# A hybrid MLA and GLA step on one core: decode's products in whole groups, and the prompt's P v in two products with the row sums on GpSimd

## The chip, the cores and the metric

The kernel runs on one core of a Trainium2 chip. The metric is the device time of one execution in microseconds (us), as the median of several runs. The core has five engines that each take their own instructions in order: PE (TensorE, matrix products; its weight loads are listed apart as PEld), DVE (VectorE), ACT (ScalarE), POOL (GpSimd) and SP (SyncE, which issues most of the transfers). They wait for each other by semaphores. Products land in PSUM, a small memory of 8 banks of 128 x 512 f32 numbers, everything else is in SBUF.

## The reference

One layer of a decoder runs for a prompt of 2048 tokens and for 8 sequences of 8 new tokens with 4096 cached positions each. The parts that matter here are the two attentions of the MLA heads:

```python
# prompt: 8 heads, 64 + 32 wide queries and keys, 64 wide values, causal
s = (jnp.einsum('bqhd,bkhd->bhqk', qn_b, k_nope)
     + jnp.einsum('bqhr,bkr->bhqk', qr_b, k_rope)).astype(jnp.float32) * scale
s = jnp.where(kpos[None, :] <= qpos[:, None], s, -jnp.inf)
p = jax.nn.softmax(s, axis=-1).astype(v.dtype)
return jnp.einsum('bhqk,bkhd->bqhd', p, v)

# decode, per sequence: pages of 128 cached latents (128 wide) and rotary keys (32 wide)
c = jnp.concatenate([ckv_pool[pages].reshape(-1, KV_LORA), cn.astype(ckv_pool.dtype)], axis=0)
kr = jnp.concatenate([kr_pool[pages].reshape(-1, QK_ROPE), krn.astype(kr_pool.dtype)], axis=0)
s = (jnp.einsum('thc,lc->htl', ql, c)
     + jnp.einsum('thr,lr->htl', qr, kr)).astype(jnp.float32) * scale
s = jnp.where(mask[None], s, -jnp.inf)
p = jax.nn.softmax(s, axis=-1).astype(c.dtype)
return jnp.einsum('htl,lc->thc', p, c)
```

Around them stand the input projection, the gated linear attention (GLA), the gates, the output projection, a second gated projection and the norms.

## The kernel before

The program is a sequence of stages: the input projection (up to about 354 us), GLA (to about 753 us), then the prompt's attention with decode woven in (to about 1183 us), the prompt's attention alone (to about 1394 us), its last head, among which the output's weights are already loaded and split (to about 1467 us), and the output.

Products in f32 precision are made of products of a faster type, `fp32r`. A number is split into a leading part, which is the number as written in that type, and a rest (`split`: ACT or GpSimd writes the leading part, DVE subtracts it, at L59 and L60; the helper `gcopy` at L51 is the GpSimd form). A product is then three products: leading by leading, leading by rest, rest by leading.

**The prompt's attention** (`attention`) goes head by head, and in a head unit by unit, j = 3, 2, 1, 0. A unit is 512 queries against their 4j + 4 blocks of 128 keys, one block a step. There are 40 steps to a head. The last four of each unit are on the diagonal: they cover 512, 384, 256 and 128 of the queries and are masked. A step is:

- three products of keys and queries into one PSUM tile `psC` (L940, L941, L942), of which there are two;
- two exponentials by ACT from it, into `ph` as the leading part of P (L944) and into `pf` in full (L946);
- a subtraction by DVE, `pl` = `pf` − `ph` (L948), both read from SBUF;
- on the diagonal two selects by GpSimd, which zero the masked part of `ph` and `pl` (L951);
- three products into the unit's tile `poC`, one bank of PSUM: leading values and a block of 64 columns of ones by `ph` (L953), the values' rest by `ph` (L954), leading values and ones by `pl` (L955). Rows 0 to 63 of `poC` are the output, and rows 64 to 127, by the ones, the sums of P over the keys.

A tile `VT` holds, for each key block, 64 columns of the values' rest, 64 of their leading part and 64 of ones. Between the steps of one unit stand the products, reductions and the transposition that find the row maxima of the next one (L910; DVE's L912, L915, L917; L925, L926). At a unit's end ACT copies `poC` out (L958), and the output and the sums go to memory (`Od`, `Dd`). The sums are later read back as `rcC`, inverted and written as `Rd`. The output stage reads this, and GpSimd multiplies it onto the gates (L1067).

**Decode** (`decode`) goes in 16 chunks, two for each of 8 sequences. A chunk's cached latents are loaded twice, by pages through SP (`ct`, and `kt` for the rotary keys) and row by row by indirect transfers that GpSimd issues (`cr`, L760). A chunk then is: four products of latents (L768) and two of rotary keys (L771) into a tile `ptD` of two banks; DVE's maximum (L774); ACT's exponential over 1024 columns (L779); eight transposes into the next `ptD` (L789); copies out of it, half by ACT (L792) and half by DVE (L793); 16 products P by latents into `poD` (L798). In the trace each product of decode is two records, a transpose one. `ptD` and `poD` have one buffer each. PSUM's eight banks are so shared as 2 (`ptD`), 1 (`poD`), 2 (`pmC`, the maxima), 2 (`psC`) and 1 (`poC`).

What sets the order: both attentions are generators, advanced in turn at a fixed rate. The framework then schedules all instructions by its own model of the machine's time and emits one fixed order for each engine. A wait on an engine therefore holds all that stands behind it.

## Time and profile before

| | us |
|---|---|
| runs (3) | 1921.84 median, 1916.32 to 1924.11 |
| profiled execution, own time | 1924.76 |
| its span | 1923.0 |
| stage: attention with decode, 753 to 1183 | 430 |
| stage: attention alone, 1183 to 1394 | 211 |
| stage: last head, 1394 to 1467 | 73 |
| stage: output, 1467 to 1923 | 456 |
| PE / DVE / ACT / POOL busy over the span | 1792.7 / 1093.2 / 777.2 / 472.6 |

The mean granted PE clock of the profiled execution is 0.959 of full speed. In the rows of the profile, L940 is line 940 of the kernel. A group's row tells line, engine, operation, the tiles it writes and reads with shapes, and its count; then its busy time in us and the mean of one in ns; then how long the engine stood idle ahead of these instructions, and for what. Products overlap on PE, so the mean of one is longer than the distance from one to the next. The stages' limits were read from the timeline.

### The profile page before, as it was taken

What the parts mean: (1) busy time and instruction counts of PE and PEld (TensorE: products, weight loads), DVE (VectorE), ACT (ScalarE), POOL (GpSimd) and SP (SyncE); (2) the same over time, 40 slices, a digit from 0 to 9 for tenths busy, and PEclk for the clock granted to TensorE, in tenths of its full rate; (3) what the DMA queues carried; (4) which work ended last, traced back from release to release, by engine and by line L of the source; (5) the groups of instructions that cost most, each with busy time, mean ns of one, the idle gap of its engine ahead of it and who ended that gap; (6) DMA issues with size and microseconds to landing.
All of it is one profiled execution on the core that took longest, in us unless ns stands there. A gap on an engine that the chain in (4) does not pass through costs nothing.

```text
span 1923.0 us, 27575 instructions
## 1 busy us (share of the span) xinstructions
PE 1792.7 (93%) x8928; PEld 1367.0 (71%) x8928; DVE 1093.2 (57%) x2373; ACT 777.2 (40%) x1896; POOL 472.6 (25%) x851
## 2 busy tenths in 40 slices
PE   4999987899999995997999999999998999999997
PEld 3877776688777784564665657777776888888885
DVE  6366566566734766555655667777786433333324
ACT  4354455344332432352543546666662122212112
POOL 5263342334433332121021111111126200000000
PEclk7999999899989998898998999999998999999999
DMA  5164476511111107446344452233134332222210
GB/s 167 47 228 164 145 262 212 136 39 38 48 34 41 45 23 184 155 124 171 106 131 128 121 160 64 72 86 75 44 102 139 102 94 82 85 81 79 77 48 33
DMA packets 197994, 200.56 MB, mean 104 GB/s; under 512 B 26362, under 2 KB 141932, under 8 KB 197852
## 3 DMA queue, kind: packets, MB, share of 16 engines
q1 hardware_dynamic: 193244, 182.03, 32.4%
q0 software_dynamic: 4608, 16.78, 2.7%
q8 instruction: 71, 1.16, 0.3%
q14 instruction: 71, 0.58, 0.1%
HBM read 142.39 MB, written 56.35 MB: 103 GB/s over the span
## 4 chain that ended last, share of the span: by engine, by line
PE 69%; DMA 4%; DVE 3%; issue 1%; POOL 1%; SPq 1%; ACT 1%; POOLq 0%; ACTq 0%; DVEq 0%
PE pgE L63 7%; PE pgE L65 7%; PE pgE L64 7%; PE pgB L65 4%; PE pgB L63 4%; PE pgB L64 4%; PE psC L940 3%; PE poC L953 3%; PE poC L955 3%; PE pmC L910 3%; PE psC L941 3%; PE psC L942 3%; PE poC L954 3%; PE ptD L768 2%; PE poD L798 2%; PE ptD L771 1%
## 5 line engine op out<-in xcount | busy, mean ns | idle before, releaser
L944 ACT ACTIVATE ph<-psC 128x512 fp32r<-128x512 f32 (+1 forms) x320 | 171.6, 536 | 262.4 <-PE psC L942 187.9
L948 DVE TENSOR_TENSOR pl<-pf,ph 128x512 fp32r<-128x512 f32 (+1 forms) x320 | 192.0, 609 | 69.7 <-ACT pf L946 63.5
L946 ACT ACTIVATE pf<-psC 128x512 f32<-128x512 f32 (+1 forms) x320 | 170.5, 533 | 0.0
L912 DVE TENSOR_REDUCE mxC<-pmC 128x1 f32<-128x512 f32 x192 | 129.1, 684 | 66.0 <-PE pmC L910 65.2
L951 POOL TENSOR_SCALAR_AFFINE_SELECT ph<-ph 128x128 fp32r<-128x128 f32 x128 | 44.7, 349 | 429.3 <-DVE pl L948 322.3
L953 PE MATMUL poC<-ph,VT 128*128 128x512 f32 (+1 forms) x320 | 125.9, 393 | 9.1 <-POOL ph L951 7.4
L910 PE MATMUL pmC<-KT,qC 96*128 96x512 f32 (+2 forms) x320 | 121.4, 403 | 8.5 <-issue 4.1
L940 PE MATMUL psC<-qC,KT 97*128 97x512 f32 (+1 forms) x320 | 126.3, 395 | 2.0 <-ACT pf L946 1.2
L955 PE MATMUL poC<-pl,VT 128*128 128x512 f32 (+1 forms) x320 | 123.5, 387 | 1.8 <-DVE pl L948 1.5
L941 PE MATMUL psC<-qC,KT 96*128 96x512 f32 (+1 forms) x320 | 120.1, 375 | 0.0
L942 PE MATMUL psC<-qC,KT 96*128 96x512 f32 (+1 forms) x320 | 119.7, 374 | 0.0
L954 PE MATMUL poC<-ph,VT 128*64 128x512 f32 (+1 forms) x320 | 117.6, 368 | 0.0
L953 PEld LDWEIGHTS poC<-ph,VT 128*128 128x128 f32 x320 | 62.1, 194 | 40.4 <-POOL ph L951 14.0
L64 PE MATMUL pgE<-wpg,hh 128*128 128x512 f32 x224 | 87.7, 391 | 0.0
L63 PE MATMUL pgE<-wpg,hh 128*128 128x512 f32 x224 | 87.6, 391 | 0.0
L1124 DVE SCALAR_TENSOR_TENSOR thE<-thE,pgE 128x512 f32<-128x512 f32 x32 | 22.0, 687 | 114.3 <-ACT thE L1123 114.2
L910 PEld LDWEIGHTS pmC<-KT,qC 96*128 96x128 f32 x320 | 62.4, 198 | 33.9 <-issue 14.2
L940 PEld LDWEIGHTS psC<-qC,KT 97*128 97x128 f32 x320 | 62.0, 194 | 33.8 <-ACT pf L946 7.7
L65 PE MATMUL pgE<-wpg,hl 128*128 128x512 f32 x224 | 85.4, 392 | 0.0
L1123 ACT ACTIVATE thE<-pgE 128x512 f32<-128x512 f32 x32 | 19.1, 598 | 161.1 <-PE pgE L65 161.1
L955 PEld LDWEIGHTS poC<-pl,VT 128*128 128x128 f32 x320 | 61.9, 193 | 24.1 <-issue 5.9
L60 DVE TENSOR_TENSOR x<-x 128x512 fp32r<-128x512 f32 (+2 forms) x74 | 64.7, 920 | 22.2 <-PE pgB L64 14.1
(450 smaller groups left out, 4643.5 us busy)
## 6 DMA issues: line engine op xcount, KB each, us to landing
x<-in_xT SPq DMA_DIRECT2D x32, 512.0 KB
ct<-in_ckvT SPq DMA_DIRECT2D x256, 64.0 KB
x<-in_w_in SPq DMA_DIRECT2D x16, 512.0 KB
Qn<-qq SPq DMA_DIRECT2D x16, 512.0 KB
Kn<-qq SPq DMA_DIRECT2D x16, 512.0 KB
Vd<-qq SPq DMA_DIRECT2D x16, 512.0 KB
KT<-Kn SPq DMA_DIRECT2D x32, 256.0 KB
VT<-Vd SPq DMA_DIRECT2D x8, 1024.0 KB
```

The source lines that it names most:

```text
L63: T_.matmul(out, ah, bh, start=first, stop=False)
L64: T_.matmul(out, ah, bl, start=False, stop=False)
L65: T_.matmul(out, al, bh, start=False, stop=last)
L910: T_.matmul(ps[:, :w], qs, kv[0][cb][:96, 0, :w], start=True, stop=True)
L940: T_.matmul(ps[:, c0:], kh[:, ks], qh[:, c0:], start=True, stop=False)
L941: T_.matmul(ps[:, c0:], kh[:96, ks], ql[:, c0:], start=False, stop=False)
L942: T_.matmul(ps[:, c0:], kl[:, ks], qh[:96, c0:], start=False, stop=True)
L944: A.activation(ph[:, c0:], ps[:, c0:], AF.Exp, scale=SC)
L948: V.tensor_tensor(pl[:, c0:], pf[:, c0:], ph[:, c0:].bitcast(F32), op=ALU.subtract)
L953: T_.matmul(o[:, c0:], vt[:, kb, DV:192], ph[:, c0:], start=kb == 0, stop=False)
L954: T_.matmul(o[:DV, c0:], vt[:, kb, 0:DV], ph[:, c0:], start=False, stop=False)
L955: T_.matmul(o[:, c0:], vt[:, kb, DV:192], pl[:, c0:], start=False, stop=kb == nk - 1)
```

## The change

There are three parts.

**Decode.** A new helper, `together`, keeps the instructions of a group in the order in which they are written and asks for all but the first at high priority. Decode's six QK products, its eight transposes and its 16 P products are each written as such a group. The QK group's order of halves is reversed. The pool `poD` is gone: everything of decode that went there now takes a buffer of `ptD`, of which there is still one. The transposes are copied out by one ACT copy of 1024 columns.

**The prompt's attention.** `poC` is now two banks, still with one buffer. One product of a step is the whole of the values, rest and leading part, by `ph` into the first bank; the second is leading values and ones by `pl` into the second bank. The sums of `ph`, which the ones gave before, are made by GpSimd in a tile `sumC` (two buffers): a copy in a unit's first step, then one addition per step. The second exponential overwrites the scores in `psC`; `pf` is gone, and DVE subtracts with one operand in PSUM. At a unit's end ACT copies half of the first bank, DVE copies the second, DVE and GpSimd each make one addition of 64 rows, `sumC` is split, two products with ones sum it over the 128 partitions, and DVE adds the result to the row that goes to `Dd`.

**The output.** It has two buffers in place of three in the pool `ptE` and six in place of five in `pgE`.

```diff
+    def together(calls):
+
+        for n, f in enumerate(calls):
+            if n:
+                with tc.high_priority():
+                    tc.keep_in_program_order(f())
+            else:
+                f()
...
         pt = pool(c, "ptD", 1, PSUM)
-        po = pool(c, "poD", 1, PSUM)
...
         def chunk(b, ck, ct, kt, cr, mx, dn, oc):
             ps = pt.tile([P, 2, 512], F32, name="ptD")
-            for u in range(2):
-                for e in range(2):
-                    T_.matmul(ps[64 * e:64 * e + 64, u], flat(qlat[:, b]), ct[:, u, e], start=True, stop=False)
-            for u in range(2):
+
+            def latent(u, e):
+                return T_.matmul(ps[64 * e:64 * e + 64, u], flat(qlat[:, b]), ct[:, u, e], start=True, stop=False)
+
+            def rope(u):
                 rows = slice(64 * u, 64 * u + 64)
-                T_.matmul(ps[:, u], qrs[rows, b].rearrange("p e h t -> p (e h t)"), kt[rows], start=False, stop=True)
+                return T_.matmul(ps[:, u], qrs[rows, b].rearrange("p e h t -> p (e h t)"), kt[rows], start=False, stop=True)
+
+
+            together([partial(latent, u, e) for u in (1, 0) for e in (1, 0)] + [partial(rope, u) for u in (1, 0)])
             yield
...
-            for k in range(8):
-                T_.transpose(tp[:, k * P:(k + 1) * P], sv[:, k], ident)
+            together([partial(T_.transpose, tp[:, k * P:(k + 1) * P], sv[:, k], ident) for k in range(8)])
             pT = sp.tile([P, 8, 2, SD], F32, name="pT")
-            pv = pT.rearrange("p k e q -> p (k e q)")
-            A.activation(pv[:, :512], tp[:, :512], AF.Copy)
-            V.tensor_copy(pv[:, 512:], tp[:, 512:])
+            A.activation(pT.rearrange("p k e q -> p (k e q)"), tp, AF.Copy)
             yield
-            oo = po.tile([P, 512], F32, name="poD")
-            for k in range(8):
-                for e in range(2):
-                    T_.matmul(oo[64 * e:64 * e + 64, :CL], pT[:, k, e], cr[:, e, k], start=k == 0, stop=k == 7)
+            oo = pt.tile([P, 2, 512], F32, name="ptD")[:, 0]
+            together([partial(T_.matmul, oo[64 * e:64 * e + 64, :CL], pT[:, k, e], cr[:, e, k], start=k == 0, stop=k == 7)
+                      for k in range(8) for e in range(2)])
...
         def attend(h, j, kv, q):
             (kt, vt), qt = kv, q
             qh, ql = qt[:, 0], qt[:96, 1]
-            o = po.tile([P, 512], F32, name="poC")
+            o = po.tile([P, 2, 512], F32, name="poC")
+            sm = sp.tile([P, 512], F32, name="sumC")
             nk = 4 * j + 4
...
                 A.activation(ph[:, c0:], ps[:, c0:], AF.Exp, scale=SC)
-                pf = pp.tile([P, 512], F32, name="pf")
-                A.activation(pf[:, c0:], ps[:, c0:], AF.Exp, scale=SC)
+                A.activation(ps[:, c0:], ps[:, c0:], AF.Exp, scale=SC)
                 pl = pp.tile([P, 512], F32R, name="pl")
-                V.tensor_tensor(pl[:, c0:], pf[:, c0:], ph[:, c0:].bitcast(F32), op=ALU.subtract)
+                V.tensor_tensor(pl[:, c0:], ps[:, c0:], ph[:, c0:].bitcast(F32), op=ALU.subtract)
...
-                T_.matmul(o[:, c0:], vt[:, kb, DV:192], ph[:, c0:], start=kb == 0, stop=False)
-                T_.matmul(o[:DV, c0:], vt[:, kb, 0:DV], ph[:, c0:], start=False, stop=False)
-                T_.matmul(o[:, c0:], vt[:, kb, DV:192], pl[:, c0:], start=False, stop=kb == nk - 1)
+                T_.matmul(o[:, 0, c0:], vt[:, kb, 0:P], ph[:, c0:], start=kb == 0, stop=kb == nk - 1)
+                T_.matmul(o[:, 1, c0:], vt[:, kb, DV:192], pl[:, c0:], start=kb == 0, stop=kb == nk - 1)
+
+                if kb == 0:
+                    gcopy(sm, ph.bitcast(F32))
+                else:
+                    G.tensor_tensor(sm[:, c0:], sm[:, c0:], ph[:, c0:].bitcast(F32), op=ALU.add)
                 yield
             ob = sp.tile([P, 512], F32, name="ob")
-            A.activation(ob, o, AF.Copy)
+            A.activation(ob[:DV], o[DV:P, 0], AF.Copy)
+            oc = sp.tile([P, 512], F32, name="oc")
+            V.tensor_copy(oc, o[:, 1])
+            V.tensor_tensor(ob[:DV], ob[:DV], o[:DV, 0], op=ALU.add)
+            G.tensor_tensor(ob[:DV], ob[:DV], oc[:DV], op=ALU.add)
             nc.sync.dma_start(Od[h * DV:(h + 1) * DV, j * 512:j * 512 + 512], ob[:DV])
-            nc.sync.dma_start(Dd[h:h + 1, j * 512:j * 512 + 512], ob[DV:DV + 1])
+
+            sr = sp.tile([P, 2, 512], F32R, name="sr", bufs=1)
+            split(sr[:, 0], sr[:, 1], sm)
+            st = pm.tile([P, 512], F32, name="pmC")
+            for l in range(2):
+                T_.matmul(st[:DV], vt[:, 0, P:192], sr[:, l], start=l == 0, stop=l == 1)
+            V.tensor_tensor(oc[DV:DV + 1], oc[DV:DV + 1], st[0:1], op=ALU.add)
+            nc.sync.dma_start(Dd[h:h + 1, j * 512:j * 512 + 512], oc[DV:DV + 1])
...
-            pt = pool(c, "ptE", 3, PSUM)
+            pt = pool(c, "ptE", 2, PSUM)
...
-            pg = pool(c, "pgE", 5, PSUM)
+            pg = pool(c, "pgE", 6, PSUM)
```

The framework moves the instructions accordingly. Up to about 753 us the order is the same on each engine. The lines of the changed kernel are about ten higher: L940 to L942 are L950 to L952, L953 is L962, L955 is L963, L768 and L771 are L777 and L781, L910 is L919, L951 is L960, L51 is L52, L1067 is L1091; L82 is the product that `together` calls, L968 the addition to `sumC`, and L975 the addition of 64 rows.

First, PE where decode's QK products of one chunk stand among attention, before (in brackets the semaphores that an instruction waits for):

```order
L798 MATMUL poD<-cr,pT 64x128 x3
L768 MATMUL ptD<-ct,qlat 64x512 [waits DMAHW4_49,DMAHW2_49,DMAHW6_49,DMAHW0_49,PE_49]
L768 MATMUL ptD<-ct,qlat 64x512 [waits DMAHW4_49,DMAHW6_49,DMAHW2_49,DMAHW0_49]
L768 MATMUL ptD<-ct,qlat 64x512
L940 MATMUL psC<-qC,KT_6769 128x512 [waits Activation_49]
L941 MATMUL psC<-qC,KT_6769 128x512
L942 MATMUL psC<-qC,KT_6769 128x512
L768 MATMUL ptD<-ct,qlat 64x512 [waits DMAHW4_49,DMAHW6_49,DMAHW2_49,DMAHW0_49]
L771 MATMUL ptD<-kt,qrs 128x512 [waits DMAHW5_49,DMAHW7_49,DMAHW3_49,DMAHW1_49] x2
```

and the like place after:

```order
L963 MATMUL poC<-pl,VT_6777 128x512 [waits DVE_49]
L950 MATMUL psC<-qC,KT_6770 128x512
L951 MATMUL psC<-qC,KT_6770 128x512
L952 MATMUL psC<-qC,KT_6770 128x512
L777 MATMUL ptD<-ct,qlat 64x512 [waits DMAHW4_49,DMAHW2_49,DMAHW6_49,DMAHW0_49,DVE_49]
L777 MATMUL ptD<-ct,qlat 64x512 x3
L781 MATMUL ptD<-kt,qrs 128x512 [waits DMAHW5_49,DMAHW7_49,DMAHW3_49,DMAHW1_49]
L781 MATMUL ptD<-kt,qrs 128x512
```

The six products now stand together, and the first one waits for all of the latents, and for DVE.

Second, PE in attention alone, between full steps of a unit, before:

```order
L910 MATMUL pmC<-KT_6771,qC 128x512 [waits DVE_49]
L955 MATMUL poC<-pl,VT_6778 128x512 [waits DVE_49]
L953 MATMUL poC<-ph,VT_6778 128x512 [waits Activation_49]
L954 MATMUL poC<-ph,VT_6778 64x512
L940 MATMUL psC<-qC,KT_6774 128x512 [waits Activation_49]
L941 MATMUL psC<-qC,KT_6774 128x512
L942 MATMUL psC<-qC,KT_6774 128x512
```

and after:

```order
L963 MATMUL poC<-pl,VT_6778 128x512 [waits DVE_49]
L962 MATMUL poC<-ph,VT_6778 128x512 [waits Activation_49]
L950 MATMUL psC<-qC,KT_6774 128x512
L951 MATMUL psC<-qC,KT_6774 128x512
L952 MATMUL psC<-qC,KT_6774 128x512
L919 MATMUL pmC<-KT_6773,qC 128x512 [waits DVE_49]
L919 MATMUL pmC<-KT_6774,qC 128x384 [waits DVE_49,PE_49]
```

L954 is gone, and the QK products, which waited for ACT's second exponential, now have their wait in the product by `pl` ahead of them, which waits for DVE's subtraction.

Third, GpSimd in the last head, where a unit's selects and the multiplication of the gates (`raw`) stand, before:

```order
L951 AFFINE_SELECT ph<-ph 128x128 [waits DVE_49]
L951 AFFINE_SELECT pl<-pl 128x128 [waits PE_49]
L1067 TENSOR_TENSOR raw<-raw 128x512 [waits DMAHW6_49,DMAHW7_49,DMAHW2_49,DMAHW0_49]
L951 AFFINE_SELECT ph<-ph 128x128 [waits DVE_49,Pool_49]
L951 AFFINE_SELECT pl<-pl 128x128 [waits PE_49,Pool_49]
```

and after:

```order
L968 TENSOR_TENSOR sumC<-sumC,ph 128x512 [waits Activation_49,Pool_49]
L975 TENSOR_TENSOR ob<-ob,oc 64x512 [waits DMAHW0_49,DVE_49]
L968 TENSOR_TENSOR sumC<-sumC,ph 128x512 [waits Activation_49,Pool_49] x5
L1091 TENSOR_TENSOR raw<-raw 128x512 [waits DMAHW5_49,DMAHW4_49,DMAHW3_49]
L968 TENSOR_TENSOR sumC<-sumC,ph 128x512 [waits Activation_49,Pool_49]
L960 AFFINE_SELECT ph<-ph 128x128 [waits DVE_49]
L960 AFFINE_SELECT pl<-pl 128x128 [waits PE_49]
```

The multiplication, which waits for transfers, now also has additions to `sumC` behind it in GpSimd's queue, and these share the queue with the selects.

13 lines of the change are left out of this document (7 added, 6 removed).

## The prediction

> **What bounds the kernel now.** I read the page's totals first, then the busy time by stage, then the groups and the timeline of the attention stage, then the chain of waits where decode runs. Totals:
>
> ```profile
> span 1923.0 us, 27575 instructions
> PE 1792.7 (93%) x8928; PEld 1367.0 (71%) x8928; DVE 1093.2 (57%) x2373; ACT 777.2 (40%) x1896; POOL 472.6 (25%) x851
> ```
>
> PE is busy 93% of the span. By stage (stretch, its length, then busy time and count of PE, PEld, DVE, ACT, POOL, then PE's granted clock, DMA share, GB/s): decode among attention, attention alone, the last head, the output.
>
> ```profile
> 753.00:1183.00 430.00, 398.91 (x1982) 249.53 (x1983) 254.79 (x755) 187.90 (x411) 60.81 (x136) 0.92 0.47 133
> 1183.00:1394.00 211.00, 207.74 (x1046) 164.84 (x1045) 161.73 (x415) 144.35 (x307) 33.52 (x120) 1.00 0.28 70
> 1394.00:1467.00 73.00, 64.10 (x278) 48.04 (x276) 54.56 (x115) 42.44 (x90) 27.81 (x48) 0.90 0.33 95
> 1467.00:1923.00 456.00, 442.05 (x1998) 358.73 (x1997) 171.05 (x243) 89.88 (x189) 52.13 (x88) 0.98 0.28 82
> ```
>
> Attention alone is PE's: 207.74 of 211 us (98%). In the decode stage PE has 31 us idle and a clock of 0.92. The output stage is PE's too. How many attention steps (one key block of one unit) fall in each of the first three stretches, the same view of L953's matmuls tells, one per step:
>
> ```profile
> 753.00:1183.00 430.00, 57.90 (x141) 27.44 (x142) 0.92 0.47 133
> 1183.00:1394.00 211.00, 51.25 (x139) 26.17 (x139) 1.00 0.28 70
> 1394.00:1467.00 73.00, 16.72 (x40) 8.48 (x40) 0.90 0.33 95
> ```
>
> 141 + 139 + 40 = 320 = 8 heads of 40 steps. Alone, a head costs 211 × 40/139 = 60.7 us.
>
> **The third product goes.** A head's 40 steps hold 28 of 512 columns and four each of 384, 256 and 128, on average 435. What one product takes is its distance to the next. One step in the timeline (start, duration):
>
> ```profile
> 1241.52 0.39 PE L940 MATMUL psC<-qC,KT 97*128 97x512 f32 x1
> 1241.75 0.40 PE L941 MATMUL psC<-qC,KT 96*128 96x512 f32 x1
> 1242.41 0.60 ACT L944 ACTIVATE ph<-psC 128x512 fp32r<-128x512 f32 x1 [0.32 <-PE psC L942]
> 1242.91 0.59 ACT L946 ACTIVATE pf<-psC 128x512 f32<-128x512 f32 x1
> 1243.53 0.69 DVE L948 TENSOR_TENSOR pl<-pf,ph 128x512 fp32r<-128x512 f32 x1 [0.47 <-ACT pf L946]
> ```
>
> 0.23 us for 512 columns, so 0.197 for 435. Two new products per unit for the sums cost 0.46. A head therefore gives PE 40 × 0.197 − 4 × 0.46 = 6.0 us less: 60.7 becomes 54.7, if PE stays the bound.
>
> **Whether it stays the bound** depends on three other engines and a ring of two buffers. The groups of attention alone:
>
> ```profile
> L948 DVE TENSOR_TENSOR pl<-pf,ph 128x512 fp32r<-128x512 f32 x94 | 63.5, 686 | 19.7 <-ACT pf L946 17.9 <-issue 1.4
> L912 DVE TENSOR_REDUCE mxC<-pmC 128x1 f32<-128x512 f32 x85 | 56.5, 683 | 14.3 <-PE pmC L910 14.3
> L944 ACT ACTIVATE ph<-psC 128x512 fp32r<-128x512 f32 x94 | 56.4, 600 | 50.2 <-PE psC L942 31.7 <-PE poC L954 15.9 <-POOL ph L951 1.3
> L951 POOL TENSOR_SCALAR_AFFINE_SELECT ph<-ph 128x128 fp32r<-128x128 f32 x60 | 19.1, 318 | 185.8 <-DVE pl L948 139.3 <-DVE mxC L904 41.8 <-PE pmC L910 4.8
> L958 ACT ACTIVATE ob<-poC 128x512 f32<-128x512 f32 x15 | 9.1, 608 | 0.2
> ```
>
> ACT hardly matters: 144.35 us here is 41.5 per head, and four splits of 0.6 make it 44. DVE's 161.73 us is 46.5 per head; each unit now adds a copy, an addition, the split's subtraction (0.69 each) and a one-row addition of 512 columns (no row shows it; I take 0.58, and at the 0.69 of a full tile it would be 0.4 more per head): 2.65 × 4 = 10.6, so 57. GpSimd gets a new task, and no row shows this addition in this stage. The nearest rows:
>
> ```profile
> L507 POOL TENSOR_TENSOR gtB<-gtB,gon 128x512 f32<-128x512 f32 x16 | 20.8, 1298 | 23.3 <-DVE gtB L506 23.3
> L179 POOL TENSOR_TENSOR acc<-acc,sq 128x512 f32<-128x512 f32 x28 | 41.7, 1489 | 11.6 <-ACT sq L175 10.3
> L51 POOL TENSOR_SCALAR x<-x 128x512 fp32r<-128x512 f32 x32 | 21.2, 679 | 64.8 <-DMA x<-in_xT 63.2 <-PE pgB L64 0.8 <-DVE wg L135 0.7
> L60 DVE TENSOR_TENSOR x<-x 128x512 fp32r<-128x512 f32 x64 | 61.2, 1000 | 17.5 <-PE pgB L64 14.1 <-ACT x L59 3.4
> L60 DVE TENSOR_TENSOR qq<-pq,qq 128x512 fp32r<-128x512 f32 x48 | 32.7, 687 | 29.8 <-ACT qq L59 29.6
> ```
>
> An in-place 128x512 f32 addition or product took GpSimd 1.30 in one stage and 1.49 in another. I take 1.30 and keep 1.49. Per head: 24 full additions 31.2, 12 narrow ones 8.8 (1.30 × 0.75, 0.5, 0.25 and some fixed cost), four copies at 0.68 = 2.7, 32 selects at 0.31 = 10, four final additions 5.2: 58 us. So PE, DVE and GpSimd would stand at 54.7, 57 and 58 per head, and none has slack to absorb a wait.
>
> The two L60 rows show that the same subtraction on VectorE takes 1.00 with both operands in SBUF and 0.69 with one in PSUM, which is the form that L948 takes now. The Trainium skill ("SBUF — State Buffer", Who interferes with whom) says that VectorE's second SBUF operand goes through a port that it shares with GpSimd, one at a time. The trace bears that out only so far: L948, with both in SBUF, already takes 0.686 beside a mostly idle GpSimd. By that rule the additions would stay near 1.30, and by the pair L179 and L507 they could be at 1.49, which is the second rival's case. A second rule speaks against the change: the same skill ("GPSIMD Engine Reference", 3. Performance versus the Vector engine) gives GpSimd 2.6 cycles an element against VectorE's one; an estimate from it is 1.1 us and a fixed cost for 512 columns, and the traced 1.30 agrees.
>
> The ring: psC has two buffers, and now one comes free only when the subtraction ends, as it is its operand. From the timeline: QK start to first exponential 0.89, to the second 0.50, that one 0.59, to the subtraction 0.03, which takes 0.69; then 0.05 for the signal and the 0.23 of the product put ahead: 3.0 us for two steps, 1.50 each. No row shows an exponential written back into PSUM; I take 0.59, bounded by the 0.50 spacing. A full step before was 7 × 0.23 = 1.62 (three QK, three P v, a maximum). So a full step can gain only 0.12: 24 per head make −2.9, not the 6.0 of PE.
>
> Against this, unit ends get longer. Before, one copy (0.61) freed the bank. Now ACT's copy (0.6) and DVE's copy (0.69) run side by side and DVE's addition (0.69) follows, about +0.8; PE stands in order at the sums product until the last addition on GpSimd, then ACT's and DVE's half of the split, about +0.25. Times four, +4.2. Net: 62.0 us per head, between 54.7 (PE's demand) and about 67 (GpSimd at 1.49 is 24 × 1.49 + 10 + 2.7 + 10 + 6 = 65, with its waits). 139 steps are 3.475 heads: **+4.5**, bounds −21 and +22.
>
> **Decode stage.** The third product goes in 141 steps: −27.8; 14 units' sums: +6.5. Decode's own products now are
>
> ```profile
> L768 PE MATMUL ptD<-ct,qlat 128*64 128x512 f32 x128 | 48.4, 654 | 14.5 <-DMA ct<-in_ckvT 9.5 <-DMA kt<-in_kropeT 4.4 <-DMA KT<-Kn 0.7
> L798 PE MATMUL poD<-cr,pT 128*64 128x128 f32 x512 | 46.4, 284 | 1.1 <-ACT pT L792 1.1
> L771 PE MATMUL ptD<-kt,qrs 64*128 64x512 f32 x64 | 31.1, 672 | 0.0
> L789 PE MATMUL ptD<-ident,sc 128*128 128x128 f32 x128 | 18.2, 282 | 0.2 <-ACT sc L779 0.2
> ```
>
> 144.1 us together. Where chance left groups whole, the chain of waits shows their price (start, length, count):
>
> ```profile
> 843.49 1.87 PE ptD L768 x8
> 845.36 1.06 PE ptD L771 x4
> 815.67 0.89 PE ptD L789 x8
> 849.88 1.45 PE poD L798 x22
> ```
>
> A chunk is 8, 4, 8 and 32 such records: 1.87 + 1.06 + 0.89 + 32/22 × 1.45 = 5.9, times 16 is 95: −49. Each entry and exit of an insert also costs, as PE's timeline at 1051 shows:
>
> ```profile
> 1051.64 0.40 PE L942 MATMUL psC<-qC,KT 96*128 96x512 f32 x1
> 1051.88 0.40 PE L910 MATMUL pmC<-KT,qC 96*128 96x512 f32 x1
> 1052.20 0.43 PE L798 MATMUL poD<-cr,pT 128*64 128x128 f32 x2
> 1052.57 0.49 PE L955 MATMUL poC<-pl,VT 128*128 128x512 f32 x1
> 1052.99 0.44 PE L798 MATMUL poD<-cr,pT 128*64 128x128 f32 x4
> ```
>
> L910 to L798 is 0.32 where 0.23 is usual, and as much is lost behind (two records of 64 rows take 0.37 to L955): some 0.2 per insert. In the order of the instructions decode's four kinds of product stand in 145 separate runs before and in 80 after: −13. In all −84 at most. Not all can be had: the rows' busy time overlaps the insert cost, the loads must come faster, and a chunk's four groups now pass through one PSUM buffer, each hand-over waiting for these:
>
> ```profile
> L774 DVE TENSOR_REDUCE m<-ptD 128x1 f32<-128x1024 f32 x16 | 19.6, 1224 | 30.7 <-PE ptD L771 30.7
> L779 ACT ACTIVATE sc<-ptD,nm 128x1024 f32<-128x1024 f32 x16 | 17.9, 1119 | 1.4 <-DVE nm L776 0.7 <-DVE mxD L782 0.6
> ```
>
> The copy of the transposes, 1024 wide on ACT, takes as long as that exponential (1.12, before two halves side by side). With the 5.9 of PE this chain (5.9 + 1.22 + 2 × 1.12) is 9.4 of a chunk's 430/16 = 27 us, so covered as long as PE's order leaves room; PE in order waits where it doesn't. I take 60%: **−50**, bounds −84 and −25 (the removed product alone, whose −21 net is sure of PE's time, and a little of the grouping).
>
> **Last head.** GpSimd also multiplies gates here, waiting for loads that come after the row sums:
>
> ```profile
> POOL raw L1067 <- DMA raw<-Rd: 14.5, 2, 13.6
> ```
>
> One such wait was 13.6 us. Before, selects queued behind it; now the running sums do as well, one per step, with the sums buffers two deep and PE's sums product behind the last of them. The chain to the reciprocal is also longer, by split, product and one-row addition (about 2 us). **+7**, bounds 0 and +15. Elsewhere nothing: the order is the same on all engines up to 753 us, and the output (442 of 456 us PE) only trades one PSUM buffer between two pools: 0, ±3.
>
> Sum: −50 + 4.5 + 7 = −38 against the span of 1923.0, so 1885. The profiled execution itself took 1924.76 and the runs' median is 1921.84; on their scale **1884**. By the bounds −84 − 21 − 3 = 1815 and −25 + 22 + 15 + 3 = 1938; the forecast's own range is 1850 to 1912.
>
> **Rivals.** *PE gets all of it* (chance 0.17). For: PE is 98% busy alone. Against: the ring's 1.50. Decode −84, attention −21, last head 0: 1818.
>
> *GpSimd decides* (0.17, slower). The selects that PE's P v products wait for stand in GpSimd's queue behind additions; with 1.49 per addition a head needs 65 us of GpSimd and, since the queue then never empties, about 68 by its waits for DVE. It decides from about 1.40 per addition, where its 58 + 28 × 0.10 = 61 passes today's 60.7. Attention +25, last head +18, and the decode stage, which does the same steps, only −33: +10, 1932. For: L179's row. Against: L507's, and that its selects cost 0.31 unhindered.
>
> *The decode stage doesn't yield* (0.16). The loads' waits in L768's row (14.5 us of idle time) and the hand-overs pace it, and grouping only moves the wait: −15 there, 1919. Against: DMA share 0.47, and 398.91 of 430 us are PE's.
>
> **How the numbers follow.** The forecast has 0.50. A measurement tells about 0.5% (10 us) from no change. Faster by more: nearly all of 0.50, all of 0.17, a little of the third rival, 0.69. Within: most of the third, some of the forecast's upper end, 0.15. Slower: 0.16 from GpSimd. The range 1828 to 1934 leaves out the far half of the first rival and a third of the GpSimd case.
>
> **What would show it.** Steps per head alone near 62 us. GpSimd's sums (L968) near 1.30; at 1.45 or more the rival holds. PE's QK waiting for DVE's subtraction every other step; at unit ends PE waiting for ACT and DVE. Decode's four groups whole at 1.87, 1.06, 0.89, 2.1. Fewer than 400 us for the stage of 753. In the last head GpSimd's wait at L1091, with additions behind. I am wrong if a head comes below 57 (the ring doesn't bind) or above 66, or if the decode stage gains less than 25.

## The result and the profile after

The changed kernel takes 2101.65 us (median of 4 runs, 2099.14 to 2106.11) against 1919.87 us before: a ratio of 1.0941, 95% interval 1.0914 to 1.0967. It is 182 us slower where 38 us faster was forecast, and far above the range's 1934. Totals of its page, then busy time by stage as before (decode among attention, attention alone, the last head, the output):

```profile
span 2097.4 us, 27553 instructions
PE 1828.7 (87%) x8672; PEld 1370.6 (65%) x8672; DVE 1192.4 (57%) x2485; ACT 807.3 (38%) x1928; POOL 851.2 (41%) x1203
```

```profile
753.00:1193.00 440.00, 352.31 (x1794) 223.58 (x1793) 275.62 (x747) 189.60 (x401) 209.83 (x270) 0.85 0.45 127
1193.00:1530.00 337.00, 278.62 (x1016) 190.69 (x1012) 227.97 (x519) 172.71 (x357) 215.29 (x297) 0.83 0.19 48
1530.00:1628.00 98.00, 72.98 (x244) 51.63 (x242) 66.96 (x127) 45.09 (x92) 71.66 (x90) 0.76 0.23 63
1628.00:2097.00 469.00, 443.99 (x1998) 358.27 (x1998) 170.53 (x248) 89.02 (x188) 57.35 (x89) 0.98 0.27 80
```

The same view of L962's products gives the steps of the second stretch:

```profile
1193.00:1530.00 337.00, 62.80 (x153) 33.31 (x153) 0.83 0.19 48
```

No engine is full in attention alone: PE 83%, DVE 68%, POOL 64%. A head takes 337 × 40/153 = 88.1 us. PE has one product less a step and yet is busy for 1.82 us a step (278.62/153) where it was 1.49 (207.74/139), at a granted clock of 0.83 in place of 1.00. In time, the last head begins 135.5 us later than before (its first product by `ph` at 1529.8 against 1394.3), takes 23.4 us more (95.8 against 72.4), and what follows it 15.5 more (471.8 against 456.3): the spans' 174.4. The groups of the attention stretches together:

```profile
L968 POOL TENSOR_TENSOR sumC<-sumC,ph 128x512 f32<-128x512 f32 x192 | 246.7, 1285 | 174.1 <-ACT ph L954 166.7 <-DMA kt<-in_kropeT 2.5 <-DMA ct<-in_ckvT 1.5
L957 DVE TENSOR_TENSOR pl<-psC,ph 128x512 fp32r<-128x512 f32 x224 | 153.3, 685 | 99.3 <-ACT psC L955 97.6 <-POOL sumC L968 0.8 <-PE poC L962 0.3
L919 PE MATMUL pmC<-KT,qC 96*128 96x512 f32 x224 | 114.9, 551 | 40.8 <-DVE mxC L921 34.0 <-issue 4.5 <-DVE mxC L926 1.3
L950 PE MATMUL psC<-qC,KT 97*128 97x512 f32 x224 | 103.7, 463 | 15.0 <-DVE pl L957 11.2 <-ACT qC L935 2.6
```

GpSimd's addition takes 1.285 us, as forecast, and the subtraction 0.685. What is new is in the third row: PE waits for VectorE's reductions at the products of the maxima, 34 us in this row and 55.7 over all widths. Two of these waits, 14.2 and 16.1 us, lie in the decode stretch. VectorE itself stands there at the inverse of a head's sums until their transfer has landed:

```profile
930.24 0.94 DVE L990 RECIPROCAL rcC<-rcC 16x128 f32<-16x128 f32 x1 [13.85 <-DMA rcC<-Dd]
1064.10 0.94 DVE L990 RECIPROCAL rcC<-rcC 16x128 f32<-16x128 f32 x1 [18.74 <-DMA rcC<-Dd]
```

Before, VectorE's longest wait at the inverse was 2.0 us. Most of the other 25 us lie at the heads' ends, as PE's timeline shows. First before (unit j = 0's last P v, then the next head's first), then after:

```profile
1331.32 0.27 PE L955 MATMUL poC<-pl,VT 128*128 128x128 f32 x1
...
1333.44 0.45 PE L953 MATMUL poC<-ph,VT 128*128 128x512 f32 x1
```

```profile
1424.57 0.41 PE L963 MATMUL poC<-pl,VT 128*128 128x128 f32 x1
1424.91 1.22 PE L919 MATMUL pmC<-KT,qC 96*128 96x512 f32 x2
1426.49 1.18 PE L919 MATMUL pmC<-KT,qC 96*128 96x512 f32 x2 [0.36 <-DVE mxC L921]
1429.48 1.26 PE L919 MATMUL pmC<-KT,qC 96*128 96x512 f32 x2 [1.81 <-DVE mxC L921]
...
1434.22 1.40 PE L919 MATMUL pmC<-KT,qC 96*128 96x512 f32 x2 [0.18 <-DVE mxC L921]
1436.89 0.59 PE L934 MATMUL pmC<-identr,m4r 128*1 128x128 f32 x4 [1.27 <-DVE mxC L913]
1437.27 1.06 PE L982 MATMUL pmC<-sr,VT 128*64 128x512 f32 x2
...
1441.73 0.63 PE L962 MATMUL poC<-ph,VT 128*128 128x512 f32 x1
```

Before, 2.1 us lie between these two; after, 17.2. For the first 12 us of it PE does nothing but the next head's maxima, two products at a time, at the pace of VectorE's 0.68 us reductions. I call the time from a unit's last product by `ph` to the next unit's first a gap. By the starts of these products heads 5 and 6, which run without decode, are:

| kernel | head, us | steps of the units | the 3 gaps inside | gap to the next head |
|---|---|---|---|---|
| before | 60.6, 60.9 | 51.6, 51.8 | 6.8, 6.8 | 2.2, 2.2 |
| changed | 89.1, 88.1 | 61.9, 57.8 | 10.0, 12.1 | 17.4, 18.3 |

The clock falls, too. The 13 us of maxima, the next 8 us, and the rest of the new unit:

```profile
1424.00:1437.00 13.00, 8.77 (x18) 4.21 (x18) 10.55 (x28) 1.11 (x2) 2.83 (x4) 0.50 0.47 129
1437.00:1445.00 8.00, 8.00 (x23) 5.83 (x21) 4.26 (x8) 3.23 (x6) 1.90 (x2) 0.51 0.01 2
1445.00:1468.00 23.00, 20.72 (x87) 14.08 (x85) 14.18 (x32) 14.63 (x31) 17.20 (x21) 1.00 0.05 12
```

PE runs at half clock in the first two stretches, though it is busy without a break in the second: 23 products in 8 us, where 0.23 us a product would make 34. The half clock did not begin with the gap: it was granted from 1421.0 to 1444.8, so from before the unit's end, where PE had just stood still for 1.5 us. The Trainium skill ("TensorE: Matmul & The Clock Gate", Part 1) says that the clock is halved after an idle window of about 3.4 us, and that some 3.4 us of sustained activity release it. The trace shows half the clock, but no pause as long as that ahead of it; and at the four heads' ends between 1260 and 1530 us the full clock came 5.2 to 8.3 us after PE's last pause.

### The profile page after: what moved, and what is told of

The parts are those of the page before. It is cut to its first block, busy times and chain, and to the rows that moved or that the text cites. A ratio compares the mean times of both kernels' runs of the same rounds, so it can differ in the third digit from the quotient of the medians.

```text
span 2097.4 us, 27553 instructions
## 1 busy us (share of the span) xinstructions
PE 1828.7 (87%) x8672; PEld 1370.6 (65%) x8672; DVE 1192.4 (57%) x2485; ACT 807.3 (38%) x1928; POOL 851.2 (41%) x1203
## 4 chain that ended last, share of the span: by engine, by line
PE 53%; DVE 12%; DMA 4%; ACT 4%; POOL 4%; SPq 3%; issue 3%; POOLq 0%; ACTq 0%; DVEq 0%
PE pgE L64 6%; PE pgE L65 6%; PE pgE L66 6%; PE pgB L66 4%; PE pgB L64 4%; PE pgB L65 4%; DVE pl L957 3%; PE poC L963 2%; DVE mxC L921 2%; PE pmC L919 2%; PE psC L950 2%; PE poC L962 2%; PE psC L951 2%; PE psC L952 2%; POOL sumC L968 2%
## 5 line engine op out<-in xcount | busy, mean ns | idle before, releaser
L968 POOL TENSOR_TENSOR sumC<-sumC,ph 128x512 f32<-128x512 f32 (+3 forms) x288 | 317.2, 1101 | 175.1 <-ACT ph L954 166.7
L954 ACT ACTIVATE ph<-psC 128x512 fp32r<-128x512 f32 (+1 forms) x320 | 170.2, 532 | 285.2 <-PE psC L952 224.1
L957 DVE TENSOR_TENSOR pl<-psC,ph 128x512 fp32r<-128x512 f32 (+1 forms) x320 | 193.5, 605 | 130.5 <-ACT psC L955 127.0
L919 PE MATMUL pmC<-KT,qC 96*128 96x512 f32 (+2 forms) x320 | 140.2, 490 | 62.7 <-DVE mxC L921 55.7
L955 ACT ACTIVATE psC<-psC 128x512 f32<-128x512 f32 (+1 forms) x320 | 169.4, 529 | 0.0
L950 PE MATMUL psC<-qC,KT 97*128 97x512 f32 (+1 forms) x320 | 137.0, 428 | 30.7 <-DVE pl L957 26.2
L963 PE MATMUL poC<-pl,VT 128*128 128x512 f32 (+1 forms) x320 | 140.4, 441 | 21.8 <-DVE pl L957 19.4
L1091 POOL TENSOR_TENSOR raw<-raw 128x512 f32<-128x512 f32 (+1 forms) x17 | 21.3, 1253 | 313.3 <-DMA raw<-Rd 313.3
L919 PEld LDWEIGHTS pmC<-KT,qC 96*128 96x128 f32 x320 | 72.5, 230 | 113.0 <-DVE mxC L921 82.1
L962 PE MATMUL poC<-ph,VT 128*128 128x512 f32 (+1 forms) x320 | 133.9, 419 | 9.3 <-POOL ph L960 4.5
L951 PE MATMUL psC<-qC,KT 96*128 96x512 f32 (+1 forms) x320 | 128.5, 401 | 0.0
L952 PE MATMUL psC<-qC,KT 96*128 96x512 f32 (+1 forms) x320 | 127.9, 400 | 0.0
L963 PEld LDWEIGHTS poC<-pl,VT 128*128 128x128 f32 x320 | 68.5, 214 | 62.3 <-DVE pl L957 49.0
L950 PEld LDWEIGHTS psC<-qC,KT 97*128 97x128 f32 x320 | 67.1, 210 | 60.3 <-DVE pl L957 41.5
L962 PEld LDWEIGHTS poC<-ph,VT 128*128 128x128 f32 x320 | 68.2, 213 | 31.9 <-POOL ph L960 9.1
L61 DVE TENSOR_TENSOR x<-x 128x512 fp32r<-128x512 f32 (+2 forms) x74 | 64.8, 921 | 22.7 <-PE pgB L65 14.2
```

What stands on the lines that cost most here:

```text
L919: T_.matmul(ps[:, :w], qs, kv[0][cb][:96, 0, :w], start=True, stop=True)
L950: T_.matmul(ps[:, c0:], kh[:, ks], qh[:, c0:], start=True, stop=False)
L951: T_.matmul(ps[:, c0:], kh[:96, ks], ql[:, c0:], start=False, stop=False)
L954: A.activation(ph[:, c0:], ps[:, c0:], AF.Exp, scale=SC)
L957: V.tensor_tensor(pl[:, c0:], ps[:, c0:], ph[:, c0:].bitcast(F32), op=ALU.subtract)
L962: T_.matmul(o[:, 0, c0:], vt[:, kb, 0:P], ph[:, c0:], start=kb == 0, stop=kb == nk - 1)
```

## The experiments

Runs 1, 3, 5 to 10, 13 and 14 were timed once, the others 4 to 12 times. The kernel before, timed beside them, spread from 1913.7 to 1929.5 us.

**Who holds the maxima back?** The sums product's tile `st` is taken from `pmC`, the maxima's pool, at a unit's end. A pool hands out its two buffers in the order of the program. So maxima that are written behind `st` can't be issued until the unit has ended and `sumC` is split. In the order of PE's instructions the next head's maxima begin, before, after 24 of a head's 40 steps; after, after 36 of 40, which is exactly the end of unit j = 1. Theory F is this fence, rival G is GpSimd's queue with the longer chains.

Run 1 takes out the sums product and its addition (the denominators then lack the sums of `ph`):

```diff
-            st = pm.tile([P, 512], F32, name="pmC")
-            for l in range(2):
-                T_.matmul(st[:DV], vt[:, 0, P:192], sr[:, l], start=l == 0, stop=l == 1)
-            V.tensor_tensor(oc[DV:DV + 1], oc[DV:DV + 1], st[0:1], op=ALU.add)
```

> The changed kernel without the sums product of a unit (the tile st in the pool of the maxima, its two products and the one-row addition); the split of sumC stays, and the denominators lack the sums of ph. Theory F (fence): st takes a buffer of the maxima's pool in program order, so the next-but-one unit's maxima cannot begin before a unit has ended; taken away, the gap of P v products at a head's boundary in attention alone falls from 17-18 us to 5 or less, a head from 87 to about 72 us, and the whole time from 2100 to 1960-2010 us. Rival G (GpSimd and longer chains: additions in front of selects, unit ends, a ring held until the subtraction): only the product's own wait goes, 0.5 us a unit; the time stays over 2075 us and the gaps over 14 us.

Run 2 keeps all the work, but writes it one unit later, and with it the transfer of the sums and their inverse (the split's tile gets two buffers):

```diff
+            while late:
+                late.pop(0)()
             ob = sp.tile([P, 512], F32, name="ob")
...
-            st = pm.tile([P, 512], F32, name="pmC")
...
+            def tail():
+                st = pm.tile([P, 512], F32, name="pmC")
...
+            if h == H - 1:
+                tail()
+            else:
+                late.append(tail)
```

> The changed kernel with the sums product of a unit written one unit later (all but the last head; the split's tile in two buffers), the same work otherwise. F: maxima may begin one unit earlier, the gaps fall to 5 us or less and the time to 1970-2020 us, near the run without the product. G: within 15 us of the changed kernel, 2085-2115 us.

Run 3 puts the fence into the kernel before:

```diff
             A.activation(ob, o, AF.Copy)
+            sr = sp.tile([P, 512], F32R, name="sr", bufs=1)
+            A.activation(sr, ob, AF.Copy)
+            st = pm.tile([P, 512], F32, name="pmC")
+            T_.matmul(st[:DV], vt[:, 0, P:192], sr, start=True, stop=True)
+            sx = sp.tile([1, 512], F32, name="sx", bufs=1)
+            V.tensor_copy(sx, st[0:1])
```

> The kernel before, with one product of the unit's copied output by the ones at each unit's end in the maxima's pool (an ACT copy, one product, one DVE copy of a row that nobody reads; the output is unchanged). F: the maxima are held to their own unit, heads alone go from 60.7 to 72-76 us by a gap of 13 us or more at the boundary, the time to 1985-2030 us. G: no more than the added work where it is not hidden, under 1945 us.

| run | us | maxima begin after | gap at the head's end | head, us |
|---|---|---|---|---|
| changed | 2101.65 | 36 of 40 | 17.4, 18.3 | 89.1, 88.1 |
| 1 | 2036.2 | 16, 15 | 3.7, 4.5 | 82.3, 81.0 |
| 2 | 2017.6 | 28 | 6.1, 6.1 | 78.9, 80.0 |
| before | 1921.5 | 24 | 2.2, 2.2 | 60.6, 60.9 |
| 3 | 2013.3 | 38 | 20.0, 17.9 | 78.2, 76.3 |

Run 2's ratio to before is 1.0492 (1.0453 to 1.0531). F holds in both directions: late, the same work is 84 us faster; and one fenced product costs the kernel before 92 us (1921.5 in that comparison), with its unit times unchanged (51.6 us a head) and all of it in one gap. Some 10 of the 84 us go with the inverse, which run 2 writes later, too: PE's two long waits behind it are 10.1 and 9.9 us there, where they were 14.2 and 16.1. In run 3 the end of a head reads like that of the changed kernel:

```profile
1376.90 0.32 PE L955 MATMUL poC<-pl,VT 128*128 128x128 f32 x1
1377.13 1.10 PE L910 MATMUL pmC<-KT,qC 96*128 96x512 f32 x2
...
1389.32 1.39 PE L910 MATMUL pmC<-KT,qC 96*128 96x512 f32 x2 [0.19 <-DVE mxC L912]
1391.99 0.59 PE L925 MATMUL pmC<-identr,m4r 128*1 128x128 f32 x4 [1.28 <-DVE mxC L904]
...
1396.83 0.63 PE L953 MATMUL poC<-ph,VT 128*128 128x512 f32 x1
```

Run 2 lies within F's time, with gaps of 6 us where 5 were expected. Run 1 does not: it should have taken 2010 us at most, and is slower than run 2 with less work and earlier maxima. Some 100 us are not the fence.

**Decode alone** is run 4: the kernel before with the changed decode; attention and output as before.

> The kernel before with the changed decode alone (pinned groups, all in ptD, one ACT copy); attention and output as before. The prediction's terms for the grouping, -49 and -13 at most, taken at 60%: about -37, so 1885 us. If loads and hand-overs pace the stage: -15 or less, 1905 us or more. If the single PSUM buffer costs more than the grouping gives: over 1930 us.

1913.66 us, ratio 0.9957 (0.9939 to 0.9975): 8 us faster. The groups did what was said, though less. Decode's products in this run (those of `together` have the lines 82 and 84):

```profile
L777 PE MATMUL ptD<-ct,qlat 128*64 128x512 f32 x128 | 36.5, 698 | 6.2 <-DMA ct<-in_ckvT 6.2
L82 PE MATMUL ptD<-cr,pT 128*64 128x128 f32 x480 | 31.4, 274 | 0.0
L781 PE MATMUL ptD<-kt,qrs 64*128 64x512 f32 x64 | 19.0, 672 | 0.0
L82 PE MATMUL ptD<-ident,sc 128*128 128x128 f32 x112 | 15.5, 280 | 0.0
L84 PE MATMUL ptD<-cr,pT 128*64 128x128 f32 x32 | 6.9, 298 | 0.0
L84 PE MATMUL ptD<-ident,sc 128*128 128x128 f32 x16 | 4.8, 298 | 0.0
```

114.1 us in place of 144.1. Of these 30 us, 22 don't arrive. A new wait in decode's stretch is PE's for a subtraction, while VectorE stands at the inverse of a head's sums for their transfer:

```profile
PE poC L964 <- DVE pl L957: 25.9, 2, 16.8
```

```profile
DVE rcC L975 <- DMA rcC<-Dd: 36.8, 3, 20.8
```

It is the wait that the changed kernel has, too. In runs 3, 7 and 8, which have the decode of before, VectorE's longest wait at the inverse is 5.6 us; in the runs with the changed decode it is 5.3 to 23.5 us as long as SyncE issues the transfers.

**The other parts of the attention's change**, runs 5 to 8. R: the ring of two `psC` buffers, held until the subtraction. S: GpSimd's additions. U: unit ends.

Run 5 is run 2 with a tile of its own for the second exponential:

```diff
-                A.activation(ps[:, c0:], ps[:, c0:], AF.Exp, scale=SC)
+                pf = pp.tile([P, 512], F32, name="pf")
+                A.activation(pf[:, c0:], ps[:, c0:], AF.Exp, scale=SC)
...
-                V.tensor_tensor(pl[:, c0:], ps[:, c0:], ph[:, c0:].bitcast(F32), op=ALU.subtract)
+                V.tensor_tensor(pl[:, c0:], pf[:, c0:], ph[:, c0:].bitcast(F32), op=ALU.subtract)
```

> The changed kernel with the late sums product (2017.6 us), and the second exponential again written to a tile pf of its own, so that psC comes free as before (the split's tile back to one buffer, for room). Theory R (ring): what is left of the loss, some 100 us, is mostly psC held until the subtraction; then 1965 us or less, with PE's QK products no longer waiting for DVE. Theory S (GpSimd's additions ahead of selects, and ph held until they are done) or U (unit ends with a copy, two additions and a split): within 20 us of 2017.

Run 6 is run 2 without the additions:

```diff
-                if kb == 0:
+                if kb == nk - 4:
                     gcopy(sm, ph.bitcast(F32))
-                else:
-                    G.tensor_tensor(sm[:, c0:], sm[:, c0:], ph[:, c0:].bitcast(F32), op=ALU.add)
```

> The same kernel with the late sums product, without GpSimd's running additions: one copy of a unit's first diagonal block of ph stands for the sums, so the denominators are left wrong; split, sums product and unit end stay. S: 1975 us or less, and selects wait only for DVE. R or U: within 20 us of 2017.

Run 7 is the kernel before with the reverse of run 5's edit, run 8 the kernel before with the lines that run 6 takes out.

> The kernel before with the second exponential in place in psC and pf gone, nothing else. By the prediction's ring, 1.50 us a step against 1.62 of PE's seven products: no change, 1910-1935 us. R: 1950 us or more.

> The kernel before with GpSimd's copy and running additions of ph as in the changed kernel, whose result nobody reads; the third product stays and nothing else waits for the sums. S: 1950 us or more, by ph held three buffers deep and selects behind additions. R or U: 1910-1935 us. The addition itself is expected at 1.29 us.

| run | us | head, us | units | gaps, all four |
|---|---|---|---|---|
| 2 | 2017.6 | 78.9, 80.0 | 62.5, 63.7 | 16.4, 16.4 |
| 5 | 2048.5 | 84.6, 84.4 | 60.0, 61.0 | 24.6, 23.5 |
| 6 | 1969.8 | 71.9, 71.6 | 57.4, 57.1 | 14.5, 14.6 |
| 7 | 1990.1 | 75.1, 75.1 | 62.3, 62.5 | 12.8, 12.6 |
| 8 | 1973.0 | 67.1, 67.2 | 59.2, 60.1 | 7.9, 7.1 |

S holds: 48 us less without the additions, 52 us more with them (runs 7 and 8 against 1921 us). One way in which they cost time is in ScalarE's row of run 2, which waits 22.2 us for a buffer of `ph` that an addition still reads:

```profile
L956 ACT ACTIVATE ph<-psC 128x512 fp32r<-128x512 f32 x224 | 133.7, 597 | 203.9 <-PE psC L954 159.5 <-POOL sumC L970 22.2 <-issue 9.9
```

R as I had put it falls in run 5, which got slower by 31 us. A reason shows in the groups of run 5, and of run 8, where the subtraction also has both operands in SBUF:

```profile
L971 POOL TENSOR_TENSOR sumC<-sumC,ph 128x512 f32<-128x512 f32 x192 | 286.7, 1493 | 76.3 <-ACT ph L956 69.0 <-issue 0.2
L960 DVE TENSOR_TENSOR pl<-pf,ph 128x512 fp32r<-128x512 f32 x224 | 234.6, 1057 | 28.4 <-ACT pf L958 26.2 <-PE psC L954 0.7 <-POOL ph L963 0.4
```

```profile
L960 POOL TENSOR_TENSOR sumC<-sumC,ph 128x512 f32<-128x512 f32 x192 | 282.0, 1469 | 102.4 <-ACT ph L945 95.6
L949 DVE TENSOR_TENSOR pl<-pf,ph 128x512 fp32r<-128x512 f32 x224 | 231.4, 1041 | 44.3 <-ACT pf L947 35.7 <-PE poC L956 5.2 <-ACT ph L945 1.6
```

The subtraction goes from 0.685 to 1.04-1.06 us and the addition from 1.285 to 1.47-1.49. In run 9 (below), which has the same subtraction and no additions, it takes 0.709:

```profile
L960 DVE TENSOR_TENSOR pl<-pf,ph 128x512 fp32r<-128x512 f32 x224 | 158.2, 709 | 40.6 <-ACT pf L958 37.9 <-PE psC L954 0.8
```

The Trainium skill ("SBUF — State Buffer", Who interferes with whom) states that a VectorE instruction with two SBUF inputs contends with a GpSimd instruction that reads SBUF. The traces agree: with one operand in PSUM the two engines kept 0.685 and 1.285. So the in-place form buys GpSimd's additions room. Its price, in an order of its own, is run 7's: 69 us, so R holds there. In it PE's waits while three heads run alone are

```profile
PE pmC L910 <- DMA qC<-Qr: 15.1, 7, 2.9
PE poC L954 <- DVE pl L947: 7.1, 9, 1.9
PE psC L940 <- DVE pl L947: 4.8, 11, 0.7
```

so PE does wait for the subtraction: in the last row at the QK products, which is the ring, and in the row above at the products by `pl`, which mostly stand ahead of them in the order. But the largest wait is another: the maxima now begin so early (after 16 of 40 steps) that their queries haven't landed.

**What the removed product is worth** and the ring with a third buffer: run 9 is run 2 with both edits (of runs 5 and 6); run 10 is run 4 in place, with its free bank as a third `psC`.

```diff
-        pS = pool(c, "psC", 2, PSUM, side="right")
+        pS = pool(c, "psC", 3, PSUM, side="right")
```

> The changed kernel with late sums product, the second exponential in a tile of its own and no running additions (one copy stands for the sums, the denominators are wrong): what is left of the attention's change is the third product's removal and the longer unit end, without fence, ring or additions. If the product's 0.197 us a step is PE's to give: 1914 - 55 (63 less 4 x 8 x 0.25), so 1855-1885 us. If the longer unit ends take it back, or PE isn't the bound: 1900 us or more.

> The kernel before with the changed decode (1914 us), whose freed bank goes to a third psC buffer, and the second exponential in place in psC. In place with two buffers cost 69 us. If it is the ring of two that costs: 1905-1935 us. If it is the in-place form itself, 1970 us or more.

Run 10: 1930.0 us, within the expected span, +16 over run 4 where two buffers cost 69. Run 9: 1954.3 us, 41 us slower than run 4. A head is 70.8 and 68.2 us; its units hold 47.0 and 45.9, 4.6 to 5.9 less than before, near the product's 6.0. The gaps hold 23.8 and 22.2 in place of 9.0. The first one in VectorE's timeline:

```profile
1289.17 0.69 DVE L960 TENSOR_TENSOR pl<-pf,ph 128x512 fp32r<-128x512 f32 x1
1290.92 0.94 DVE L994 RECIPROCAL rcC<-rcC 16x128 f32<-16x128 f32 x1 [1.07 <-DMA rcC<-Dd]
1291.79 0.62 DVE L976 COPY oc<-poC 128x512 f32<-128x512 f32 x1
1292.34 0.66 DVE L977 TENSOR_TENSOR ob<-ob,poC 64x512 f32<-64x512 f32 x1
```

PE's last product of that unit started at 1287.78, the next unit's first at 1293.14. The two operations that free the banks take 1.3 us, but stand in VectorE's order behind other work and a transfer. Over three heads alone PE's two largest waits are at the end of the maxima and, second, at this release:

```profile
PE pmC L934 <- DVE mxC L913: 9.6, 6, 3.4
PE poC L965 <- DVE ob L977: 6.7, 6, 1.9
```

Run 13 frees the banks by ScalarE (run 9's sums left out as there, and one buffer for the tile `oc`), run 14 does that in run 2, as shown:

```diff
-            oc = sp.tile([P, 512], F32, name="oc")
-            V.tensor_copy(oc, o[:, 1])
-            V.tensor_tensor(ob[:DV], ob[:DV], o[:DV, 0], op=ALU.add)
-            G.tensor_tensor(ob[:DV], ob[:DV], oc[:DV], op=ALU.add)
+            oa = sp.tile([P, 2, 512], F32, name="oc")
+            A.activation(oa, o, AF.Copy)
+            oc = oa[:, 1]
+            for l in range(2):
+                G.tensor_tensor(ob[:DV], ob[:DV], oa[:DV, l], op=ALU.add)
```

> The run without ring, fence and additions (1954 us, a head alone 70.9 us, 23 us of it gaps between units), with the two output banks copied out by ScalarE alone (a second copy, 1024 wide, some 1.1 us) and both additions of 64 rows on GpSimd; the sums are left out as there. Theory U: the gaps come from VectorE, where the copy and the addition that free the banks queue behind reductions, subtractions and a reciprocal's transfer; then the gaps fall to 14 us a head or less and the time to 1900 us or less. If the gaps are from other work at a unit's end (sum product, split), 1935 us or more.

> The changed kernel with the late sums product (2017.6 us), its output banks freed by ScalarE alone as in the other run, all sums in place. U: 1975 us or less; what then remains is the ring and GpSimd's additions. Otherwise within 20 us of 2017.

1946.0 and 2021.7 us. The gaps fell, from 23.8 and 22.2 to 17.4 and 19.3 in run 13 and from 16.4 to 12.9 and 12.5 in run 14, but units got longer (49.5 and 64.1 us), and the time hardly moved. By its own terms (gaps of 14 us or less and 1900 us in run 13, 1975 us in run 14) U falls: the release is worth 3 to 6 us of a head's gaps, and what else fills them stays open.

**A better version.** Runs 11, 12, 15 and 16 build on run 4. Run 11 writes a head's inverse one unit later, by a list like run 2's; the others give the bank that decode freed to `psC` (12), `poC` (15) or `pmC` (16), with the changed output's pools.

```diff
-                V.reciprocal(rc[:n], rc[:n])
-                nc.sync.dma_start(Rd[h, view].rearrange("(a b) -> a b", b=P), rc[:n])
+                def invert():
+                    V.reciprocal(rc[:n], rc[:n])
+                    nc.sync.dma_start(Rd[h, view].rearrange("(a b) -> a b", b=P), rc[:n])
```

> The kernel before with the changed decode, and a head's inverse of the sums written one unit later, since VectorE waited 48.7 us for the sums' transfer in that run, once 20.8, with PE behind. If this wait ate the grouping's gain: 1875-1900 us. If the grouping has no more to give: 1905 us or more.

> The same with late inverse, and the freed bank as a third psC buffer. PE is 97% busy in attention alone, so there no more than 2%; in the decode stage QK products may run one step further ahead: 5 to 15 us below the run with two buffers, or no difference if psC was never waited for.

> The kernel before with the changed decode and late inverse (1910 us), the bank that decode freed given to a second buffer of poC. The gaps between units, 9.0 us a head alone, hold about 1.3 us each beyond PE's work; 3 us a head at most can go: 1885-1905 us. If the order matters more: no better than 1910.

> The same, the bank given to a third buffer of the maxima's pool. The next head's maxima begin after 16 of a head's 40 steps in the order, against 24 before and 36 in the changed kernel. If their early start is what keeps the gap at a head's end small: that gap stays at 2 us or less and the time is 1890-1910 us; no gain if it is already hidden.

| run | us | ratio (95%) | maxima begin after | gap at the head's end |
|---|---|---|---|---|
| 11 | 1910.2 | 0.9949 (0.9934-0.9964) | 24 | 2.2 |
| 12, third psC | 1962.8 | 1.022 (1.020-1.024) | 32 | 14.8, 17.7 |
| 15, second poC | 1910.5 | 0.9944 (0.9922-0.9965) | 24 | 2.2 |
| 16, third pmC | 1943.4 | 1.0120 (1.0089-1.0151) | 16 | 1.9, 2.1 |

Runs 11 and 15 are half a per cent faster than the kernel before, as run 4 nearly was without their edits (0.9957). In run 11 VectorE's longest wait at the inverse is still 16.2 us. A spare buffer made runs 12 and 16 slower, against my expectation: the order is made anew for each kernel. In run 12 the maxima came late again, with no fence, and the gap came with them; in run 16 they came early, the gap stayed small as expected, but the other gaps and the units grew, and PE waited for queries as in run 7. Among the kernels with three products the gap at a head's end goes with the maxima's start (2 us at 24 steps or earlier, 9 at 28 in run 10, 15 and more from 32 on); the time doesn't go with it alone.

Runs 17 and 18 are run 11 and run 15 with the sums' three small transfers on ScalarE's queue, the first of which is shown, and with the read-back, too, one unit later:

```diff
-            nc.sync.dma_start(Dd[h:h + 1, j * 512:j * 512 + 512], ob[DV:DV + 1])
+            nc.scalar.dma_start(Dd[h:h + 1, j * 512:j * 512 + 512], ob[DV:DV + 1])
```

> The kernel before with the changed decode, the three small transfers of a head's row sums (Dd, rcC, Rd) issued from ScalarE's queue in place of SyncE's, load and inverse one unit later. If VectorE's wait for them ate the grouping's gain: DVE's wait at the inverse under 8 us in all, PE's wait behind it gone, the time 1880-1900 us. If the grouping is limited elsewhere: 1905 us or more with the waits gone.

> The same, with the freed bank as a second buffer of poC (1910.5 us with SyncE's queue). As the other run, and no slower than it: 1875-1900 us if the wait ate the gain, 1905 us or more otherwise.

1914.6 us (0.9957, 0.9939 to 0.9974) and 1924.7 us (1.0004, 0.9984 to 1.0023). VectorE's wait in decode's stretch fell to 11.5 us in run 17 (8 were expected) and PE's wait behind it, 26 us in run 4, went, but now ScalarE, which issues the transfers, stands for decode's loads:

```profile
ACT ph L955 <- DMA ct<-in_ckvT: 10.2, 2, 5.6
ACT oc L808 <- DMA ct<-in_ckvT: 9.7, 1, 9.7
ACT qC L935 <- DMA kt<-in_kropeT: 7.4, 1, 7.4
```

The waits moved to the engine that took the transfers. That this one wait ate the grouping's gain falls; what paces the stage stays open between loads and hand-overs.

## Why the prediction was wrong

- **Unit ends, "about +0.8 ... about +0.25 ... Times four, +4.2": the step that failed most.** I priced the sums product as a wait in PE's order, and didn't ask which buffer it takes. It shares the maxima's pool, so it fences them in. Runs 2 and 3 give the fence 84 us, some 10 of them the inverse's, and 92 us. Even without fence, ring and additions the gaps grew by 13 to 15 us a head (run 9), not 4.2. For the bank's release, which was moved into VectorE's order, I counted the durations there, not the queue; by runs 13 and 14 this is 3 to 6 us of it, and the rest is open.
- **The clock wasn't a term at all.** I took 0.23 us a product as given. At the head's end above it is 0.43 for as long as the half clock lasts. Over the span the granted clock is 0.906 in place of 0.959, so some 118 us more of full clock were withheld (0.094 × 2097 less 0.041 × 1923); as PE had nothing to do in part of that time, this is an estimate from above of what the clock cost.
- **The ring, "a full step can gain only 0.12".** The 1.50 us allowed the subtraction 0.03 us of waiting. In the changed kernel PE waits for it 41 times at the QK products and 36 times at those by `pl`, 45.6 us in 320 steps. In run 7 a unit of 16 steps takes 26.2 us in place of 24.2, and one of 8, half of it diagonal, 12.1 in place of 9.2. That the ring binds where steps are short and VectorE has reductions in between fits this, but run 7 has the waits for queries, too. Two buffers cost 69 us and three 16; since the order changed too (maxima after 16 and after 28 steps), that difference isn't the ring's alone.
- **GpSimd, "I take 1.30": right in size (1.285), wrong in effect.** The load per head (58 us) fits in 61 us, so I let it pass. Run 6 shows that the additions cost 48 us all the same, on an engine that is 71% busy (run 2, heads alone); 22.2 us of ScalarE's waiting for `ph` show it directly. The rival "GpSimd decides" had the right sign, but its condition, 1.40 and more per addition, came only in runs 5 and 8; and none of the rivals named the maxima.
- **Third product, 6.0 us a head: right** (run 9: 4.6 to 5.9 within the units), and given back in the gaps.
- **Decode, "I take 60%: -50".** The grouping's share of it would be 37. Busy time of decode's products fell by 30 of the 49 named, and 8 arrived (run 4). The third rival, at 15 or less, was right on this term, and on its mechanism in part: a wait came in its place, though at the inverse of the sums, which no term and no rival named. In the changed kernel it holds PE for 30 us. (PE's trace has decode's four kinds of product in 149 separate runs before and 64 after, where I had 145 and 80.)
- **Last head, +7:** from first to last product by `ph` 95.8 us in place of 72.4, so +23. GpSimd's wait at the gates isn't what did it, 4.0 us in place of 14.5: in 1530 to 1628 VectorE's subtraction, ScalarE and GpSimd wait for each other in turn, as in the other heads.
- **Elsewhere, "0, ±3":** what follows the last head took 15.5 us more. 3 of them are PE's wait for the last unit's sums; the rest I did not locate. The buffers traded between two pools aren't it: runs 10 and 15 have the same trade and 458 us there, 2 more than before.

The single costs (92, 69, 52, less 8) don't add up to 182, and needn't: each was measured in an order of its own, and one wait hides behind another. Run 12 shows that a new order alone, with a buffer more and the same work, can move this kernel by 50 us, so a single run's difference of that size is no clean price of its edit; the fence rests on the gaps and the order too.

## What to carry to other kernels

When a change takes a buffer from a pool that other work runs ahead in, ask what is written behind it: a tile that is released late holds back everything that rotates after it, and no duration shows that. Count how early the critical producer starts in the order, before and after; here it stood in the order of PE's instructions (24 against 36 of 40 steps) and would have warned of the fence. With one engine at 98%, moving its work to two engines at 77% and less makes their queues the new latency: ask what stands ahead of a scarce buffer's release in the queue of the engine that makes it. To give the release to another engine shortened the gaps here (runs 13 and 14), but not the time.
